# GDN mixer of a hybrid flow block on one core: k and q before v, and the gate columns as fp32 products in four column groups

## The chip, the cores and the metric

The kernel runs on one core of one Trainium2 chip. The metric is device time in microseconds (us) of one execution. Of each kernel one execution is profiled; its span runs from the first to the last instruction.

## The reference, cut to what matters

Two layers work on 512 latent and 256 context tokens of width 1024. In each layer the tokens are normalised and modulated, multiplied by one input matrix, mixed by four head groups, multiplied by an output matrix and sent through an MLP. The change lies in the first group, the bidirectional gated DeltaNet (GDN):

```
qkv = silu(dwconv_centred(concat([q, k, v]), conv_w))      # 5 taps, per channel
q, k, v = split(qkv, 3)
g = -exp(a_log) * softplus(a + dt_bias);  beta = sigmoid(b)
q, k = l2norm(q), l2norm(k)                                 # per head
# per chunk of 64 tokens: a = strict(kbeta @ k.T * decay), solve (a + I) sol = rhs, then a scan over chunks
```

So q, k and v are 256 columns each of the input product, and the gates are 16 columns (a, b) here and 16 more (input and forget gates) of the mLSTM group, which the same 32-column product makes.

## The kernel before, in words

Activations lie transposed: 128 channels on the partitions, 768 tokens along them (256 context, 512 latent). Every large product is written as three fp32r products of split operands: the weights as `whi` and `wlo`, the activations as `hhi` and `hlo` (`gemm`, `gemm_pair`; all matmuls go through the helper `mm`, L181). A block of 128 output columns takes, for 8 slices of the 1024 inputs and 2 segments of tokens (256 and 512), 3 products each. `wload` brings a weight block into one of two `wst` buffers by a DMA of the SP queue, and `wsplit` splits it, in two halves, on ACT (`whi`, L184) and DVE (`wlo`, L187).

A layer's front runs in this order of the program. `modulated` makes the eight `hhi`, `hlo` pairs from X on DVE and ACT. `gemm_pair` multiplies the gates (32 columns, out 32 partitions) and the first k block (128 columns) side by side, slice by slice, as the pairs come. The gates are copied out of PSUM, transposed by six matmuls (L639), biased, multiplied by a table of signs (L187, the constant `sgn`) and sent through a softplus in some twenty short DVE instructions on tiles of 128x192 (L649 to L664). Then a loop handles the blocks in the order k0, v0, k1, v1, q0, q1: product into two PSUM banks, copy into a padded temporary `ta` (two buffers, its borders cleared by POOL, L694 to L696), five taps (one ACT, four DVE, L190), sigmoid (one DVE, three ACT), a multiplication, and for k and q a norm over each head (`unit_rows`: square, product with `blk64`, logarithm, exponential, multiplication). At each block the next block's weights are loaded and split.

Then, for each of six chunk pairs s, `gdn_pre` builds the decays and the k by k and k by q products (`gq`), `gdn_inv` inverts a triangular matrix by five doubling steps, each a chain of small matmuls (`t`, `yt`) and DVE instructions (`T`, `Y`, `Z`), `gdn_kt` prepares keys and brings v in (`vkT`, from `vf`), and `gdn_scan` runs two steps of the scan (`rps`, `yps`, `sps`, `ops`). Behind that in program order stand the other groups' products: sk, sq, sv, the gMLP's v, lk, lq, later lv (`gemm`, `gemm_tok`), and the preparation of the mLSTM (`mb`, `aRp`, `Mt`).

What sets the order: outside one marked block late in the layer, a planner puts the instructions on each engine's queue when the program is built. It takes what is ready by its own estimate, oldest in program order first. On the chip each queue is then worked through in that fixed order, and a waiting instruction holds back those behind it. The PSUM has four general banks (`ps`) and some named ones (`gi`, `go`, `gs`). The weight splits take turns among buffers named in `wset`: two halves in `wsp`, two in `gd` (tags Y1 and Nh, later used by the inverse), and from L760 on `wsp` alone.

Of the kernel before, what the change touches and what calls it, by code (L numbers as in the profile page):

```python
# [24 lines left out]
EPS = 1e-6  # L25
NEG = -1e30
GAP = NT + 2
P1 = [1, 0, 5, 4, 3, 2]
MIXK = (4, 5, 0, 1, 6, 7, 2, 3)
ALL = ((0, 256), (256, 512))  # L30
# [13 lines left out]
def go(t):  # L44
# [2 lines left out]

_LAYOUT = (
    ("ident", 128), ("blk64", 128), ("triA", 128), ("triB", 128), ("fwd", 128), ("rev", 128), ("rot", 128),
    ("d4", 4), ("d4q", 8), ("nlo", 2), ("csel", 8), ("sgn", 32), ("eps", 1), ("odg", 64), ("half", 2),  # L50
    ("gmask", 128), ("up", 128), ("lw", 128), ("sel2", 256), ("lvl", 384),
    ("cos", 512), ("sin", 512), ("selP", 128), ("ind", 512),
)
_OFF = {}
# [9 lines left out]
def constants():  # L64

    c = np.zeros((128, NCONST), np.float32)

    def put(name, a):
        o, w = _OFF[name]
        c[:a.shape[0], o:o + w] = a  # L70

    p = np.arange(128)
    same = (p[:, None] // 64) == (p[None] // 64)
    le = p[:, None] <= p[None]
    ge = p[:, None] >= p[None]
    lo_half = p < 64
    put("ident", np.eye(128))
    put("blk64", same)
    put("triA", same & np.where(lo_half[None], le, ge))
    put("triB", same & np.where(lo_half[None], ge, le))  # L80
    put("fwd", le)
    put("rev", ge)
    rot = np.zeros((128, 128))
    for h in range(2):
        for i in range(32):
            rot[64 * h + 32 + i, 64 * h + i] = -1.0
            rot[64 * h + i, 64 * h + 32 + i] = 1.0
    put("rot", rot)
    t = np.arange(SEQ)
    inv = np.power(np.float32(10000.0), -np.arange(16, dtype=np.float32) / np.float32(16)).astype(np.float32)  # L90
    ang = np.concatenate([(t // 64).astype(np.float32)[:, None] * inv, (t % 64).astype(np.float32)[:, None] * inv], 1)
    ang = np.tile(ang.astype(np.float64).T, (4, 1))
    put("cos", np.cos(ang))
    put("sin", np.sin(ang))
    g = np.zeros((128, 2, 64))
    j, i = p[:, None] % 64, np.arange(64)[None]
    for s in range(2):
        d = (p[:, None] >= 64) ^ bool(s)
        ok = np.where(d, i <= j, i >= j)
        g[:, s] = np.where(ok, 0.0, NEG)  # L100
    put("gmask", g.reshape(128, 128))
    put("up", np.where(p[None] >= p[:, None], 0.0, NEG))
    put("lw", np.where(p[None] <= p[:, None], 0.0, NEG))
    r = np.arange(64)
    half, k8 = r // 32, r % 32
    live = k8 < 8
    put("selP", live[:, None] & ((p[None] >= 64) == half[:, None]))
    sel2 = np.zeros((64, 2, 128))
    for q in range(2):
        sel2[:, q] = live[:, None] & ((r[:, None] % 4) == 2 * q + (p[None] >= 64))  # L110
    put("sel2", np.tile(sel2.reshape(64, 256), (2, 1)))
    put("d4", live[:, None] & ((r[:, None] % 4) == np.arange(4)[None]))
    put("d4q", (k8 < 16)[:, None] & (half[:, None] == np.arange(8)[None] // 4)
        & ((r[:, None] % 4) == np.array([0, 2, 1, 3] * 2)[None]))
    put("nlo", np.where(np.stack([k8 // 4 == 1, k8 // 4 == 3], 1), -1.0, 0.0))
    c[64:128, _OFF["nlo"][0]] = np.where(k8 // 8 == 1, -1.0, 0.0)
    c[64:128, _OFF["ind"][0]:_OFF["ind"][0] + 512] = (k8[:, None] < 16) & (k8[:, None] % 8 == np.arange(512)[None] // 64)
    lv = [np.where((j // 2 == i // 2) & (j != i), -1.0 / 1024.0, 0.0)]
    for n in range(1, 6):
        b = 1 << n  # L120
        lv.append(((j // (2 * b) == i // (2 * b)) & (j // b != i // b)) / 1024.0)
    put("lvl", np.concatenate(lv, 1))
    cs = np.zeros((128, 8))
    for k in range(4):
        cs[32 * k, 2 * k] = cs[32 * k + 1, 2 * k + 1] = 1.0
    put("csel", cs)
    sg = np.ones((128, 32))
    sg[:, 8:16] = sg[:, 24:32] = -1.0
    put("sgn", sg)
    put("eps", np.full((128, 1), EPS))  # L130
    put("half", np.stack([lo_half, ~lo_half], 1))
    put("odg", np.where(j == i, 0.0, 1024.0))
    return c
# [9 lines left out]
def flow_kernel(ctx, tc, t, out, dbg=None, stop=None):  # L143
    nc = tc.nc
# [41 lines left out]
    def tt(o, a, b, op, eng=None):  # L186
        (eng or V).tensor_tensor(out=o, in0=a, in1=b, op=op)  # L187
# [39 lines left out]
    def bank(c0):  # L227
        return 0 if c0 == 0 else 1
# [53 lines left out]
    def evac(dst, o, segs, rows=128):  # L282
        for c0, cn in segs:
            act_(dst[:, c0:c0 + cn], o[bank(c0)][0:rows, 0:cn], AF.Copy)
# [224 lines left out]
    def gemm_pair(w2, acts, segs, n):  # L509
# [9 lines left out]
                           start=(k == 0 and pi == 0), stop=(k == 7 and pi == 2))  # L519
        return outs  # L520

    def gemm_tok(l, c0, pairs, hk, evac):

        outs = {}
        for j, p in enumerate(pairs):
            if j % 2 == 0:
                o = ps("mmt")
            outs[p] = (o, j)
        for kc in range(2):
            st = wst.tile([128, 8, 128], F32, tag="wst", name="wst")  # L530
            sv = st.rearrange("p k n -> p (k n)").rearrange("p (k n) -> p k n", k=4)
            nc.sync.dma_start(out=sv, in_=t["w_in"][l, 512 * kc:512 * kc + 512, c0:c0 + 256]
                              .rearrange("(k p) n -> p k n", p=128))
            hv = [[x.rearrange("p k n -> p (k n)").rearrange("p (k n) -> p k n", k=2) for x in q] for q in wsplit(st, 128)]
            for hf in range(2):
                hi, lo = hv[hf]
                for p in pairs:
                    o, j = outs[p]
                    for k in range(2):
                        kk = 4 * kc + 2 * hf + k  # L540
                        ahi, alo = hk[kk]
                        for pi, (w, a) in enumerate(((hi, ahi), (hi, alo), (lo, ahi))):
                            mm(o[:, 256 * (j % 2):256 * (j % 2) + 256], a[:, 128 * p:128 * p + 128], w[:, k, :],
                               start=(kk == 0 and pi == 0 and j % 2 == 0),
                               stop=(kk == 7 and pi == 2 and (j % 2 == 1 or p == pairs[-1])))
        for p in pairs:
            o, j = outs[p]
            evac(p, o[:, 256 * (j % 2):256 * (j % 2) + 256])
# [51 lines left out]
    for l in range(DEPTH):  # L600
# [19 lines left out]
        def z3(name, dt=F32):  # L620
            return zp.tile([128, NT], dt, tag="z3", name=name, bufs=6)

        ahead = [wload([win[:, C_AB:C_AB + 16], win[:, C_IF:C_IF + 16]]), wload([win[:, C_GK:C_GK + 128]])]
        h = modulated(l, 0, ALL, nrm, tp)
        del nrm
        xd = dp.tile([8, 128, NT], F32, tag="xd", name="xd")
# [2 lines left out]

        def temp(tag, w=GAP + 4):  # L630
            return tp.tile([128, GAP + 4], F32, tag=tag, name=tag, bufs=1 if tag == "tc" else 2)


        zg = temp("ta")
        o, o_k0 = gemm_pair(ahead, h, ALL, (32, 128))
        evac(zg[0:32], o, ALL, 32)
        o = ps("gatesT")
        for p in range(NP):
            T.transpose(o[:, 32 * p:32 * p + 32], zg[0:32, 128 * p:128 * p + 128], ident[0:32, 0:32])  # L639
        wb = z3("wb")  # L640
        ysp = z3("ysp")[:, 0:384].rearrange("p (x s g) -> p x s g", x=2, s=6)
        y, sp = ysp[:, 0], ysp[:, 1]
        u = temp("tb")[:, 0:192].rearrange("p (s g) -> p s g", g=32)
        w = temp("tc")[:, 0:192].rearrange("p (s g) -> p s g", g=32)
        tt(y, o[:, 0:192].rearrange("p (s g) -> p s g", g=32), bc(tokp[l][:, 0:32], 1, 6), ADD)
        tt(y, y, bc(cc("sgn"), 1, 6), MUL)
        nega = tokp[l][:, 32:40]
        act_(nega, nega, AF.Exp)
        V.tensor_scalar(out=nega, in0=nega, scalar1=-1.0, scalar2=None, op0=MUL)  # L649
# [32 lines left out]
            else:  # L682
                stt(x[:, a0:], x[:, a0:], f, e[:, a0:], MUL, MUL)

        cols = [(C_GK, C_GQ, C_GV)[which] + 128 * j for which, j in ((0, 0), (2, 0), (0, 1), (2, 1), (1, 0), (1, 1))]
        ready = {}
        for i, (which, j) in enumerate(((0, 0), (2, 0), (0, 1), (2, 1), (1, 0), (1, 1))):
            qlat = which == 1 and last
            segs = LAT if qlat else ALL
            o = gemm(None, h, segs, w2=ready.pop(i)) if i else o_k0  # L690
            if i < 5:
                ready[i + 1] = wload([win[:, cols[i + 1]:cols[i + 1] + 128]])
            raw = temp("ta")
            G.memset(raw[:, 0:2], 0.0)  # L694
# [8 lines left out]
            act_(acc[:, a0:], raw[:, a0:GAP], AF.Copy, scale=prm[l][:, cw:cw + 1])  # L703
            for tp_ in range(1, 5):
                stt(acc[:, a0:], raw[:, a0 + tp_:GAP + tp_], prm[l][:, cw + 6 * tp_:cw + 6 * tp_ + 1], acc[:, a0:], MUL, ADD)
            e = temp("tb")[:, 0:GAP] if i % 2 else gd.tile([128, 1024], F32, tag="at", name="e", bufs=2)[:, 0:GAP]
            sigmoid_(acc[:, a0:], e[:, a0:])
            tt(acc[:, a0:], acc[:, a0:], e[:, a0:], MUL)
            if len(unit) > 2 - 1:
# [1 line left out]
            if which < 2:  # L711
                act_(e[:, a0:], acc[:, a0:], AF.Square)
                unit.append((acc, e, a0, 0.125 if which else None))
        while unit:
            unit_rows()

# [40 lines left out]
                act_(glq[hp, :, :, f, :], o[hp, q:48:2].rearrange("p (s t h) -> p s t h", s=6, t=2), AF.Exp)  # L757


        wset[:] = [(wsp, "whi", "wlo")]  # L760
        mix = [None] * 8
        O = [xm.tile([128, NT], F32, tag="xm", name="O") for _ in range(2)]
        for x in O:
# [235 lines left out]

        gdn_pre(0)  # L1000
        gdn_inv(0)
        gdn_kt(0)
        gdn_pre(1)
        gdn_inv(1)
# [632 lines left out]
```

## Time and profile before

| what | value |
|---|---|
| median of 3 runs | 1955.21 us (1955.19 to 1955.52) |
| profiled execution | 1955.14 us, span 1953.4 us, mean granted TensorE clock 0.977 |
| TensorE matmul (PE) | 1874.8 us busy, 96% of the span |
| VectorE (DVE) | 1201.8 us, 62% |
| ScalarE (ACT) | 757.4 us, 39% |
| GpSimd (POOL) | 104.6 us, 5% |
| front of layer 0, first products to the mLSTM's preparation | about 45 to 325 us |
| front of layer 1 | about 1155 to 1400 us |

PE is the matrix engine's matmuls, PEld its weight loads, which run beside them. A busy PE isn't PE at its peak, since matmuls are pipelined and a recorded duration overlaps the next one; the distance from one start to the next tells what a matmul really costs. Idle time of an engine is given with what ended it.

### The profile page before, as it was taken

What the parts mean: (1) busy time and instruction counts of PE and PEld (TensorE: products, weight loads), DVE (VectorE), ACT (ScalarE), POOL (GpSimd) and SP (SyncE); (2) the same over time, 40 slices, a digit from 0 to 9 for tenths busy, and PEclk for the clock granted to TensorE, in tenths of its full rate; (3) what the DMA queues carried; (4) which work ended last, traced back from release to release, by engine and by line L of the source; (5) the groups of instructions that cost most, each with busy time, mean ns of one, the idle gap of its engine ahead of it and who ended that gap; (6) DMA issues with size and microseconds to landing.
All of it is one profiled execution on the core that took longest, in us unless ns stands there. A gap on an engine that the chain in (4) does not pass through costs nothing.

```text
span 1953.4 us, 34015 instructions
## 1 busy us (share of the span) xinstructions
PE 1874.8 (96%) x14131; PEld 1536.4 (79%) x14131; DVE 1201.8 (62%) x2221; ACT 757.4 (39%) x1530; POOL 104.6 (5%) x169
## 2 busy tenths in 40 slices
PE   5999999999899999999999999999999999999998
PEld 3877778778777888888888878677777778888887
DVE  3978885666769557435535349798676754444443
ACT  4652343555524312313213236434255543333242
POOL 0021110000000000000000000211100000000001
PEclk8999999999799999999999999999999999999999
DMA  8321001121464345335433222210011323333332
GB/s 310 97 52 34 13 24 34 57 65 34 147 199 129 107 131 148 116 93 151 140 87 108 78 58 55 63 35 24 23 44 33 102 81 98 97 97 97 97 97 76
DMA packets 225955, 172.56 MB, mean 88 GB/s; under 512 B 19106, under 2 KB 208008, under 8 KB 225800
## 3 DMA queue, kind: packets, MB, share of 16 engines
q1 hardware_dynamic: 219424, 153.71, 26.6%
q10 hardware_dynamic: 4680, 10.64, 1.5%
q0 software_dynamic: 1696, 6.03, 0.9%
q8 instruction: 111, 1.82, 0.4%
q14 instruction: 44, 0.36, 0.1%
HBM read 163.02 MB, written 7.34 MB: 87 GB/s over the span
## 4 chain that ended last, share of the span: by engine, by line
PE 82%; DVE 9%; ACT 3%; DMA 3%; issue 1%; POOL 1%; DVEq 0%; ACTq 0%; SPq 0%; POOLq 0%
PE mm L181 64%; PE mmt L181 3%; PE num L181 1%; PE ops L181 1%; DMA wst<-w_in 1%; PE pv L181 1%; DVE wlo L187 1%; DVE Y L187 1%; PE adaps L181 1%; PE yt L181 1%; DVE kq L190 1%; PE t L181 1%; PE pT L1353 1%; DMA adw<-ada_w 1%; PE yps L181 1%
## 5 line engine op out<-in xcount | busy, mean ns | idle before, releaser
L184 ACT ACTIVATE whi<-wst 128x512 fp32r<-128x512 f32 (+1 forms) x388 | 241.9, 627 | 683.8 <-PE mm L181 628.8
L181 PE MATMUL mm<-hhi,whi 128*128 128x512 f32 (+3 forms) x1344 | 479.5, 362 | 11.7 <-ACT hhi L184 11.0
L181 PE MATMUL mm<-hlo,whi 128*128 128x512 f32 (+3 forms) x1344 | 479.3, 357 | 1.2 <-DVE hlo L190 1.1
L181 PE MATMUL mm<-hhi,wlo 128*128 128x512 f32 (+3 forms) x1344 | 476.3, 356 | 0.0
L187 DVE TENSOR_TENSOR wlo<-wst,whi 128x512 fp32r<-128x512 f32 (+1 forms) x388 | 265.7, 689 | 312.9 <-ACT whi L184 308.5
L181 PEld LDWEIGHTS mm<-hhi,whi 128*128 128x128 f32 (+1 forms) x1344 | 252.7, 189 | 55.2 <-ACT hhi L184 14.4
L181 PEld LDWEIGHTS mm<-hlo,whi 128*128 128x128 f32 (+1 forms) x1344 | 253.9, 189 | 38.0 <-DVE hlo L190 2.3
L181 PEld LDWEIGHTS mm<-hhi,wlo 128*128 128x128 f32 (+1 forms) x1344 | 253.2, 189 | 38.6 <-issue 1.5
L181 PE MATMUL mm<-fhi,whi 128*128 128x512 f32 (+1 forms) x784 | 275.9, 352 | 0.0
L181 PE MATMUL mm<-flo,whi 128*128 128x512 f32 (+1 forms) x784 | 275.8, 352 | 0.0
L181 PE MATMUL mm<-fhi,wlo 128*128 128x512 f32 (+1 forms) x784 | 274.5, 350 | 0.0
L190 DVE SCALAR_TENSOR_TENSOR x<-mm,mod,x 128x256 f32<-128x256 f32 (+1 forms) x122 | 79.6, 653 | 139.8 <-PE mm L181 139.7
L181 PEld LDWEIGHTS mm<-fhi,whi 128*128 128x128 f32 x784 | 148.3, 189 | 21.9 <-ACT r L184 0.8
L181 PEld LDWEIGHTS mm<-fhi,wlo 128*128 128x128 f32 x784 | 148.1, 189 | 19.7
L181 PEld LDWEIGHTS mm<-flo,whi 128*128 128x128 f32 x784 | 148.4, 189 | 19.1
L190 DVE SCALAR_TENSOR_TENSOR adacc<-adw,scT,adacc 128x1024 f32<-128x1024 f32 x84 | 105.9, 1282 | 28.0 <-DMA adw<-ada_w 27.9
L187 DVE TENSOR_TENSOR flo<-r,fhi 128x768 fp32r<-128x768 f32 (+1 forms) x64 | 52.6, 825 | 39.2 <-ACT fhi L184 39.1
L184 ACT ACTIVATE fhi<-r 128x768 fp32r<-128x768 f32 (+1 forms) x64 | 47.2, 740 | 65.9 <-DVE r L187 65.9
L181 PE MATMUL mm<-mlo,whi 128*128 128x512 f32 (+1 forms) x192 | 69.7, 363 | 1.3 <-DVE mlo L187 1.3
L181 PE MATMUL mm<-mhi,whi 128*128 128x512 f32 (+1 forms) x192 | 69.5, 362 | 0.4 <-ACT mhi L184 0.4
L181 PE MATMUL mm<-mhi,wlo 128*128 128x512 f32 (+1 forms) x192 | 68.8, 359 | 0.0
L184 ACT ACTIVATE r<-mm 128x256 f32<-128x256 f32 (+1 forms) x96 | 49.1, 515 | 32.2 <-PE mm L181 32.2
(406 smaller groups left out, 2712.1 us busy)
## 6 DMA issues: line engine op xcount, KB each, us to landing
wst<-mlp_w SPq DMA_DIRECT2D x128, 512.0 KB, 3.8
adw<-ada_w SPq DMA_DIRECT2D x96, 512.0 KB, 4.1
wst<-w_in SPq DMA_DIRECT2D x44, 512.0 KB, 3.7
wst<-w_out SPq DMA_DIRECT2D x64, 128.0 KB, 3.2
xd<-x ACTq DMA_DIRECT2D x8, 384.0 KB, 3.4
x<-xd POOLq DMA_DIRECT2D x8, 384.0 KB, 5.5
xs<-x ACTq DMA_DIRECT2D x4, 512.0 KB, 7.2
wst<-w_in SPq DMA_DIRECT2D x8, 256.0 KB, 3.2
```

Source lines behind the costliest of these rows:

```text
L181: T.matmul(o, lhsT=l, rhs=r, start=start, stop=stop)
L184: S.activation(out=o, in_=i, func=f, **kw)
L187: (eng or V).tensor_tensor(out=o, in0=a, in1=b, op=op)
L190: V.scalar_tensor_tensor(out=o, in0=a, scalar=s, in1=b, op0=op0, op1=op1)
L1353: T.transpose(o[:, 256 * i + 128 * g:256 * i + 128 * g + 128], Ps[g][:, 128 * (i0 + i):128 * (i0 + i) + 128], ident)
```

## The change

The order of the blocks becomes k0, k1, q0, q1 and then v0, v1. `gemm_pair` now multiplies k0 and k1 side by side while the activations are made, and the gates follow in `gemm_groups`: plain fp32 weights, not split, against `hhi` and `hlo` read as fp32, 16 products of 32 columns for each segment, dealt out to four groups of 32 output partitions. The transposition becomes six matmuls with a table `sid`, which adds the four groups and carries the signs. The sign multiplication goes, and one small DVE instruction turns the sign of eight bias columns. The loop body becomes `project(i, o)`; blocks 0 to 3 are called before the norms end, blocks 4 and 5 (v) after `gdn_inv(0)` and before `gdn_kt(0)`.

As written, q0's weights are loaded and split twice: once ahead of the gates (`ready = {2: ...}`), and once more in `project(1)`, since `0 < i < 5` holds for i = 1; the second copy is the one used.

```diff
+PROJ = ((0, 0), (0, 1), (1, 0), (1, 1), (2, 0), (2, 1))
 P1 = [1, 0, 5, 4, 3, 2]
...
+    put("sid", np.where(p[:, None] % 32 == np.arange(32)[None], np.where(np.arange(32)[None] // 8 % 2, -1.0, 1.0), 0.0))
...
+    def gemm_groups(w, acts, segs, n):
+        outs = {0: gi("mmg"), 1: go1("mmg")}
+        for c0, cn in segs:
+            for i in range(16):
+                k, a = i // 2, acts[i // 2][i % 2]
+                g = slice(32 * (i % 4), 32 * (i % 4) + n)
+                mm(outs[bank(c0)][g, 0:cn], w[:, k], a[:, c0:c0 + cn].bitcast(F32), start=i < 4, stop=i >= 12)
+        return outs
...
-        ahead = [wload([win[:, C_AB:C_AB + 16], win[:, C_IF:C_IF + 16]]), wload([win[:, C_GK:C_GK + 128]])]
+        ahead = [wload([win[:, c:c + 128]]) for c in (C_GK, C_GK + 128)]
+        w_g = gd.tile([128, 8, 64], F32, tag="E", name="w_g")[:, :, 0:32]
+        for i, c in enumerate((C_AB, C_IF)):
+            nc.sync.dma_start(out=w_g[:, :, 16 * i:16 * i + 16], in_=win[:, c:c + 16].rearrange("(k p) n -> p k n", p=128))
...
+        first = gemm_pair(ahead, h, ALL, (128, 128))
+        ready = {2: wload([win[:, C_GQ:C_GQ + 128]])}
         zg = temp("ta")
-        o, o_k0 = gemm_pair(ahead, h, ALL, (32, 128))
-        evac(zg[0:32], o, ALL, 32)
+        evac(zg, gemm_groups(w_g, h, ALL, 32), ALL)
         o = ps("gatesT")
         for p in range(NP):
-            T.transpose(o[:, 32 * p:32 * p + 32], zg[0:32, 128 * p:128 * p + 128], ident[0:32, 0:32])
+            mm(o[:, 32 * p:32 * p + 32], zg[:, 128 * p:128 * p + 128], cc("sid"))
...
+        V.tensor_scalar(out=tokp[l][:, 24:32], in0=tokp[l][:, 24:32], scalar1=-1.0, scalar2=None, op0=MUL)
         tt(y, o[:, 0:192].rearrange("p (s g) -> p s g", g=32), bc(tokp[l][:, 0:32], 1, 6), ADD)
-        tt(y, y, bc(cc("sgn"), 1, 6), MUL)
...
-        for i, (which, j) in enumerate(((0, 0), (2, 0), (0, 1), (2, 1), (1, 0), (1, 1))):
+        def project(i, o):
+            which, j = PROJ[i]
...
-            o = gemm(None, h, segs, w2=ready.pop(i)) if i else o_k0
-            if i < 5:
+            o = o or gemm(None, h, segs, w2=ready.pop(i))
+            if 0 < i < 5:
                 ready[i + 1] = wload([win[:, cols[i + 1]:cols[i + 1] + 128]])
...
-            e = temp("tb")[:, 0:GAP] if i % 2 else gd.tile([128, 1024], F32, tag="at", name="e", bufs=2)[:, 0:GAP]
+            e = temp("tb")[:, 0:GAP] if i % 2 or i > 3 else gd.tile([128, 1024], F32, tag="at", name="e", bufs=2)[:, 0:GAP]
...
+        for i in range(4):
+            if i == 3:
+                wset[:] = [(wsp, "whi", "wlo")]
+            project(i, first[i] if i < 2 else None)
         while unit:
             unit_rows()
...
-        wset[:] = [(wsp, "whi", "wlo")]
...
         gdn_pre(0)
         gdn_inv(0)
+        for i in (4, 5):
+            project(i, None)
         gdn_kt(0)
```

## Rows read from the trace of the kernel before

**Rows 1.** The page: busy time by engine, and the chain that ended last by engine.

```profile
PE 1874.8 (96%) x14131; PEld 1536.4 (79%) x14131; DVE 1201.8 (62%) x2221; ACT 757.4 (39%) x1530; POOL 104.6 (5%) x169
...
PE 82%; DVE 9%; ACT 3%; DMA 3%; issue 1%; POOL 1%; DVEq 0%; ACTq 0%; SPq 0%; POOLq 0%
```

**Rows 2.** Busy time by stretch, both fronts (length; busy us; clock; DMA share; GB/s).

```profile
65.70:138.00 72.30, 70.71 (x433) 57.72 (x433) 57.70 (x106) 48.10 (x84) 9.86 (x25) 1.00 0.25 65
138.00:309.00 171.00, 162.72 (x2581) 126.00 (x2580) 136.72 (x262) 57.76 (x142) 27.42 (x29) 0.98 0.09 24
...
1179.00:1238.00 59.00, 57.30 (x350) 46.11 (x353) 50.97 (x99) 42.23 (x75) 8.20 (x25) 1.00 0.30 78
1238.00:1405.00 167.00, 160.85 (x2542) 122.82 (x2534) 136.25 (x266) 56.56 (x131) 27.54 (x30) 0.98 0.11 31
```

**Rows 3.** PE in order of time (start, duration): the scan's end in either layer.

```profile
308.52 0.66 PE L181 MATMUL ops<-ATb,yy 128*64 128x128 f32 x8
...
321.52 0.39 PE L181 MATMUL mm<-hhi,wlo 128*128 128x512 f32 x1
...
1404.39 0.66 PE L181 MATMUL ops<-ATb,yy 128*64 128x128 f32 x8
```

**Rows 4.** PE in order of time: products of the gates, beside the first k block.

```profile
53.22 0.28 PE L181 MATMUL mm<-hlo,whi 128*32 128x256 f32 x1
53.34 0.28 PE L181 MATMUL mm<-hhi,wlo 128*32 128x256 f32 x1
53.45 0.39 PE L181 MATMUL mm<-hhi,whi 128*32 128x512 f32 x1
53.68 0.39 PE L181 MATMUL mm<-hlo,whi 128*32 128x512 f32 x1
53.91 0.39 PE L181 MATMUL mm<-hhi,wlo 128*32 128x512 f32 x1
54.14 0.28 PE L181 MATMUL mm<-hlo,whi 128*128 128x256 f32 x1
```

**Rows 5.** PE in order of time: fp32 in four groups, the transposition, small fp32 products.

```profile
14.64 1.07 PE L181 MATMUL adaps<-adw,scT 128*32 128x256 f32 x16
...
65.63 0.65 PE L639 MATMUL gatesT<-cst,ta 32*128 32x32 f32 x6
...
324.61 0.62 PE L181 MATMUL mb<-ysp,cst 128*128 128x24 f32 x4
```

**Rows 6.** Groups of instructions by shape, 42 to 127 us (count, busy us, mean ns, idle).

```profile
L187 DVE TENSOR_TENSOR wlo<-wst,whi 128x512 fp32r<-128x512 f32 x15 | 10.3, 697 | 1.1 <-ACT whi L184 1.1
L184 ACT ACTIVATE whi<-wst 128x512 fp32r<-128x512 f32 x15 | 9.2, 625 | 7.7 <-PE mm L181 6.7 <-DVE sc L254 0.9
L190 DVE SCALAR_TENSOR_TENSOR vf<-ta,prm,vf 128x770 f32<-128x770 f32 x8 | 8.1, 1014 | 2.4 <-ACT vf L184 2.4
...
L187 DVE TENSOR_TENSOR vf<-vf,tb 128x770 f32<-128x770 f32 x2 | 1.9, 954 | 0.0
...
L288 DVE TENSOR_SCALAR vf<-vf 128x770 f32<-128x770 f32 x2 | 1.1, 555 | 0.0
```

**Rows 7.** Busy time by stretch: the beginning of the execution (columns as in rows 2).

```profile
0.00:25.00 25.00, 13.71 (x98) 8.06 (x99) 5.94 (x31) 10.24 (x29) 0.35 (x6) 0.91 0.92 335
```

**Rows 8.** PE in order of time, idle time before it in brackets: GDN and mLSTM waits.

```profile
133.52 0.89 PE L181 MATMUL gq<-kq 64*64 64x128 f32 x24
...
141.02 0.59 PE L181 MATMUL t<-Z,Nh 128*128 128x64 f16 x8 [2.21 <-DVE Z L860]
...
1240.34 0.39 PE L181 MATMUL t<-Z,Nh 128*128 128x64 f16 x8 [1.94 <-DVE Z L860]
...
1414.40 0.63 PE L181 MATMUL Mt<-cst,tc 64*128 64x64 f32 x4 [1.85 <-DVE tc L1177]
```

**Rows 9.** Busy time by stretch, around two falls of the clock (columns as in rows 2).

```profile
140.00:147.00 7.00, 5.98 (x62) 4.58 (x62) 5.03 (x10) 0.72 (x2) 1.35 (x3) 0.51 0.00 0
...
1416.80:1423.60 6.80, 6.80 (x32) 6.68 (x32) 6.64 (x13) 0.49 (x2) 0.00 (x0) 0.50 0.11 24
```

More of the change, by code (lines that the diff above doesn't have):

```diff
@@ L49 @@
     ("ident", 128), ("blk64", 128), ("triA", 128), ("triB", 128), ("fwd", 128), ("rev", 128), ("rot", 128),
-    ("d4", 4), ("d4q", 8), ("nlo", 2), ("csel", 8), ("sgn", 32), ("eps", 1), ("odg", 64), ("half", 2),
-    ("gmask", 128), ("up", 128), ("lw", 128), ("sel2", 256), ("lvl", 384),
+    ("d4", 4), ("d4q", 8), ("nlo", 2), ("csel", 8), ("eps", 1), ("odg", 64), ("half", 2),
+    ("sid", 32), ("gmask", 128), ("up", 128), ("lw", 128), ("sel2", 256), ("lvl", 384),
     ("cos", 512), ("sin", 512), ("selP", 128), ("ind", 512),
@@ L126, in constants @@
     put("csel", cs)
-    sg = np.ones((128, 32))
-    sg[:, 8:16] = sg[:, 24:32] = -1.0
-    put("sgn", sg)
     put("eps", np.full((128, 1), EPS))
@@ L683, in unit_rows @@
                 stt(x[:, a0:], x[:, a0:], f, e[:, a0:], MUL, MUL)
-        cols = [(C_GK, C_GQ, C_GV)[which] + 128 * j for which, j in ((0, 0), (2, 0), (0, 1), (2, 1), (1, 0), (1, 1))]
-        ready = {}
-        for i, (which, j) in enumerate(((0, 0), (2, 0), (0, 1), (2, 1), (1, 0), (1, 1))):
+        cols = [(C_GK, C_GQ, C_GV)[which] + 128 * j for which, j in PROJ]
+        def project(i, o):
+            which, j = PROJ[i]
             qlat = which == 1 and last
             segs = LAT if qlat else ALL
-            o = gemm(None, h, segs, w2=ready.pop(i)) if i else o_k0
-            if i < 5:
+            o = o or gemm(None, h, segs, w2=ready.pop(i))
+            if 0 < i < 5:
                 ready[i + 1] = wload([win[:, cols[i + 1]:cols[i + 1] + 128]])
```

## The prediction

> **What bounds the kernel now.** I read the page first: PE is busy for 96% of the span, and the chain that ended last is 82% PE [rows 1]. Busy time alone proves little, so I then cut the two fronts that the change touches into stretches [rows 2]. In all four PE is busy 95 to 98% and DVE 80 to 86%: PE leads, and DVE is near enough behind it to matter. Last I looked for what still stands on PE's queue when the GDN chain is done, since only that tells which of the two sets the end. In layer 0 the last products of the scan start at 308.52, and block products run on without a gap to 321.52 [rows 3]: the chain ends some 13 us before its cover does. In layer 1 the scan ends at 1404.39 [rows 3], and products for lv follow it as well. So a front ends when PE has worked off its list. PE time saved counts; a GDN chain that starts sooner counts only through fewer waits of PE.
>
> **The gates' product, PE.** Before, it's 48 products a layer (8 slices, 2 segments, 3 each). From start to start one of 256 columns takes 0.12 us and one of 512 takes 0.23 [rows 4]: 24 x 0.12 + 24 x 0.23 = 8.4 us; the mean of the true distances (53.22 to 53.91 holds two of one and two of the other) makes it 8.3. This costs PE as much as a block of 128 columns would, so putting k1 in its place beside k0 costs nothing, and k1's own 8.3 us later vanish. What comes in is the group form. The trace has it already: the 16 matmuls at 14.64 are two slices of the modulation product, four groups each, and every fp32 product is recorded as two matmuls. They take 1.07 us, of which the last four outlive their start by 0.4: (1.07 - 0.4) / 3 = 0.22 us for four at once, 256 columns wide [rows 5]. The gates need 16 products a segment, so 4 rounds of two passes: 8 x 0.22 = 1.8 for 256 columns, and 8 x 0.44 = 3.5 for 512, where I double the row. Together 5.3 us. Saved: 3.0 a layer.
>
> Weighing a rule: four groups start together in that row and the next four follow 0.22 us later, which is what one pass of 256 columns costs alone (mb's four short passes start 0.12 apart, for a tenth of the columns) [rows 5], so I take full overlap. The Trainium skill, "TensorE: Matmul & The Clock Gate", Part 3 (Packing small matmuls), measured less: three column groups gave 2.38 times and four row groups 3.07 times. By 3.07 the gates would take 32 x 0.66 / 3.07 = 6.9 us and the end would come 3.2 us later than my sum, an estimate; row and rule differ, and I go by the row.
>
> **The transposition.** Six matmuls in 0.65 us become six fp32 products, twelve passes. The nearest row is mb, four passes in 0.62 with the last one's 0.27: 0.12 each [rows 5], so 12 x 0.12 = 1.4: 0.75 more. Net on PE: -2.25 a layer, **-4.5** for both. Bounds: nothing saved if the new pieces hit a wait, and -6.0 if the transposition hides.
>
> **The doubled q0 load.** 512 KB, two ACT splits of 0.63 and two DVE splits of 0.70 more a layer; the gates' two narrow splits and the sign multiplication leave DVE. DVE gains about 0.7 us of work, on an engine with 14.6 idle in 65.7 to 138 [rows 2, 6]: 0 on the path. The used copy needs k1's buffers, free only when the pair ends, and the gates' 5.3 us are its cover; without that cover it costs PE one half's split, 0.63 + 0.70 = 1.3 a layer.
>
> **Loads.** Before the first product k0 and k1 (1024 KB) must now have come, instead of k0 and the gates (640 KB); on SP's queue the small gate loads go behind. At the start DMA is 92% busy at 335 GB/s [rows 7], so layer 0 may begin 384 / 335 = 1.1 us later; the other end is -0.4, from two narrow splits that leave DVE's queue there (an estimate, a quarter of 0.70 each and up [rows 6]). I take +0.5. In layer 1 the MLP's tail covers it. The gate loads wait there for memory of the MLP and may hold q0's load behind them on SP, which isn't needed before the pair has ended.
>
> **v behind the inverse.** On PE v0 and v1 only change places. On DVE their 8.1 + 1.9 + 1.1 = 11.1 us [rows 6] leave the way to the first `gq`, now complete at 133.52 [rows 8], and fall into the first inverse; I put that 12 to 18 us earlier. Three queues feel it: v's `ta` temporaries, and POOL's clearing of them, now stand in front of the rope tables (ACT's queue), of the gMLP weights (POOL's) and beside POOL's multiplication in `gdn_pre`; v1's sigmoid needs the `tb` that q1's norm frees; k1's copy out of PSUM waits for the gates' `ta`. Behind a late v stands `gdn_kt(0)` and so the first scan step; the 12 to 18 us are its cover.
>
> What that's worth is the waits. PE stood 2.21 us for the first inverse in layer 0 and then ran 7 us at half clock (granted 0.51, the lower of its two levels), which costs 3.4 more; in layer 1 it stood 1.94 there, and 1.85 before `Mt`, after which 6.8 us at 0.50 cost 3.4 [rows 8, 9]. Together 12.8. Such waits are places where the planned order and the chip disagree; a new order moves them and makes others. Bounds -12.8 to +11.2 (one wait with its clock, 2.2 + 3.4, new in each layer). Near the middle, since old stalls may go as easily as new ones come, with a little for the earlier chain: **-1.5**.
>
> **Sum.** -4.5 + 0.5 - 1.5 = -5.5 us. The profiled execution took 1955.14 us (span 1953.4 and 1.7 around it), 0.07 below the median of the runs, so the forecast is **1949.6 us**, 0.28% less.
>
> **The rivals.**
> 1. Forecast: PE's saving arrives, waits about as many as before. Own range 1945 to 1953. Chance 0.48. For it: the block products that outlast the scan [rows 3].
> 2. The earlier chain also removes the first inverse's waits in both layers: 2.2 + 3.4 + 1.9 = 7.5 instead of 1.5: 1943.6, and to 1939 if the fall before `Mt` goes too. For it: the waits lie where the order changes. Against: PE was filled there with sk and sq already. Chance 0.18.
> 3. The saving turns into waits: DVE, 80% busy before the change and more crowded inside the first inverse, sets the pace there, and PE finishes early only to stand. Then the -4.5 is lost and about 0.5 of loads stays: 1955.6, range 1952 to 1958. Chance 0.15.
> 4. The four groups overlap only in part at 512 columns. If a round takes a third more than in rows 5, the gates take 7.1 and 0.45 a layer is left: -0.9 + 0.5 - 1.5, 1953.2. The skill's 3.07 of above is this case. The trace speaks against it. Chance 0.04.
> 5. Slower: v's products clog PSUM. Their banks can be freed only into a `ta`, and a `ta` only by taps on a DVE that now prefers the inverse; two of the four general banks stay held, the next block's product waits, and everything on PE's queue behind it. From a wait of about 2 us on the clock falls as at 140 us: 5.6 in each layer, 11.2 - 4.0 = +7.2, 1962.3. It decides when the wait exceeds 1 us a layer beyond today's. For it: DVE at 80%. Against: 14.6 us of idle DVE time ahead of the inverse, enough for v's 11.1 [rows 2, 6]. Chance 0.13.
> 6. It doesn't do what it says: the planner may issue v's products ahead of the inverse wherever PE has nothing older ready. I expect that, in part, and the sum doesn't hang on it; that v comes late on DVE neither, leaving the -4.5 + 0.5: 1951.1. Chance 0.02.
>
> **Numbers.** A measurement of this kernel can tell about 0.2%, 3.9 us, from no change. Faster by more (below 1951.3): most of case 1 (0.38), all of 2, a little of 5 and 6 (0.02): 0.58. Slower by more (above 1959.1): case 5 and a tail of 3: 0.15. The rest 0.27. The range 1941 to 1958 holds cases 1, 3, 4, 6 and most of 2, some 8 in 10.
>
> **What would show it.** Right: 64 matmuls of 128*32 in fp32 for the gates, some 5.3 us a layer between the pair and q0; `gq` of the first chunk pair some 15 us earlier in both layers; the scan's end earlier by as much, block products outlasting it longer; `mb` earlier by 2 to 4 us. Wrong: a wait of PE above 1 us between the pair and q0, or for a `ps` bank in the first inverse; DVE idle before the first `gq`; new stretches at clock 0.5; the groups' starts further apart than 0.44 at 512 columns.

## The result, and the profile after

The changed kernel is slower: 1976.58 us median of 4 runs (1973.51 to 1978.45), ratio to before 1.0106 (95% interval 1.0089 to 1.0123), so some 21 us where 5.5 less were forecast. The profiled execution took 1975.99 us, span 1974.2, which is 20.8 more than the span before.

First the page of the changed kernel, busy time and chain by engine; they answer to [rows 1].

```profile
PE 1881.2 (95%) x14175; PEld 1533.7 (78%) x14175; DVE 1202.2 (61%) x2221; ACT 760.1 (39%) x1530; POOL 102.4 (5%) x169
...
PE 84%; DVE 8%; ACT 3%; DMA 3%; issue 1%; POOL 1%; ACTq 0%; SPq 0%; POOLq 0%; DVEq 0%
```

PE has 6.4 us more busy time though its work was meant to shrink, and it is still the chain. To see where the 20.8 us arise, cut the span at events of PE. I call a layer's front the time from the first product of the new activations to the first `Mt`; idle is the time in it in which no matmul runs.

| stretch, us | before | after | difference |
|---|---|---|---|
| start to the first product | 45.9 | 46.8 | +0.9 |
| front of layer 0 (idle in it) | 289.2 (11.6) | 296.5 (17.5) | +7.3 (+5.9) |
| between the fronts | 823.2 | 827.2 | +3.9 |
| front of layer 1 (idle in it) | 256.1 (10.8) | 265.8 (18.6) | +9.7 (+7.8) |
| `Mt` of layer 1 to the end | 539.0 | 538.0 | -1.0 |

Between the fronts the two kernels do the same, and this stretch took 823 to 829 us over all profiles of this document, so the +3.9 is scatter; the two fronts carry the loss. Not all of it is idle time. TensorE's granted clock stood at its lower level, 0.50, for 12.3 and 10.2 us of the two fronts before and for 21.2 and 20.4 us after, with PE busy for 21.3 of them before and 35.8 after. If half of that busy time is lost (an estimate), the clock took 7 us more than before, and with the 13.7 us of idle time that makes 21. The fronts together grew by 17.0: twenty `mmt` products (4 us), which stood ahead of layer 1's `Mt` before, stand behind it now.

Next, PE in order of time in the changed kernel (start, duration, idle time before it in brackets): around the end of q1's product in both layers.

```profile
101.27 1.23 PE L180 MATMUL l<-e,cst 128*128 128x258 f32 x2 [4.35 <-ACT e L183]
103.07 2.07 PE L180 MATMUL l<-e,cst 128*128 128x512 f32 x2 [0.57 <-ACT e L183]
104.93 1.35 PE L180 MATMUL gc<-gtmp,cst 128*128 128x24 f32 x6
106.22 0.67 PE L180 MATMUL glps<-gtmp,ones 64*128 64x48 f32 x4
106.81 0.58 PE L180 MATMUL mm<-hhi,whi 128*128 128x256 f32 x1
...
119.38 0.89 PE L180 MATMUL gq<-kq 64*64 64x128 f32 x24 [0.31 <-DVE kq L189]
...
309.24 0.66 PE L180 MATMUL ops<-ATb,yy 128*64 128x128 f32 x8
...
332.83 0.62 PE L180 MATMUL mb<-ysp,cst 128*128 128x24 f32 x4
...
1217.96 1.04 PE L180 MATMUL l<-tb,cst 128*128 128x258 f32 x2 [5.07 <-ACT tb L183]
1220.17 2.08 PE L180 MATMUL l<-tb,cst 128*128 128x512 f32 x2 [1.17 <-ACT tb L183]
```

q1's product has ended at 94.3. Then PE's queue holds only the norms' products (`l`) and the gates' sums (`gc`, `glps`), each behind a chain of ACT and DVE, and v0 starts at 106.81 behind all of them. The first complete `gq` is at 119.38, 14.1 us earlier than in [rows 8], as forecast. But the scan ends at 309.24 where it ended at 308.52 [rows 3]: the lead is lost on the way. And `mb` comes 8.2 us later than in [rows 5]. In layer 1, counted from the front's first product, the first `gq` starts 9.8 us sooner than before and the scan's last product 4.1 us later.

Now busy time by stretch (columns as in [rows 2]), first the changed kernel: from the end of the gates' transposition to the first `t` (the inverse's first product), from there to the first `rps` (the first full scan step), in either layer; the last two rows are the two falls of the clock.

```profile
76.81:128.29 51.48, 43.77 (x235) 33.28 (x235) 40.88 (x82) 33.19 (x55) 7.09 (x20) 0.87 0.08 21
128.29:167.60 39.31, 36.73 (x421) 28.43 (x420) 35.17 (x55) 16.40 (x31) 6.83 (x9) 1.00 0.29 70
...
1200.96:1242.69 41.73, 32.59 (x160) 22.82 (x159) 34.10 (x77) 27.02 (x47) 6.64 (x20) 0.84 0.09 26
1242.69:1284.70 42.01, 39.52 (x424) 29.36 (x423) 32.96 (x53) 19.20 (x34) 7.02 (x9) 1.00 0.25 61
...
98.70:112.40 13.70, 10.56 (x41) 7.57 (x42) 10.84 (x32) 8.45 (x16) 1.12 (x4) 0.50 0.12 35
1218.30:1232.00 13.70, 11.75 (x34) 7.12 (x32) 9.93 (x35) 8.31 (x18) 1.96 (x5) 0.51 0.14 38
```

And the same four stretches of the kernel before:

```profile
66.28:141.02 74.74, 70.94 (x434) 57.50 (x434) 60.30 (x109) 47.52 (x82) 10.74 (x25) 0.99 0.25 62
141.02:172.10 31.08, 30.92 (x372) 23.67 (x371) 24.36 (x41) 7.36 (x16) 3.99 (x5) 0.90 0.13 36
...
1179.30:1240.34 61.04, 57.40 (x362) 46.21 (x362) 53.13 (x103) 42.23 (x75) 9.32 (x25) 1.00 0.29 76
1240.34:1271.50 31.16, 31.16 (x373) 22.42 (x372) 25.82 (x47) 9.59 (x18) 5.58 (x7) 1.00 0.12 35
```

Read the length less PE's busy time. Ahead of the first `t` PE stood 3.8 and 3.6 us before the change and 7.7 and 9.1 after it, and with each stall go 13.7 us at the lower clock (in layer 0 they begin within it). From `t` to the first scan step it took 31 us in both layers, and now 39 and 42: v's taps are on DVE there (busy 24.4 us before, 35.2 after).

Last, PE in order of time where products of the gates (`mmg`) run between those of the pair; and in a second fence the busy time by stretch of `mmg` alone (length; PE, weight loads, ACT's copy; clock; DMA).

```profile
51.53 0.40 PE L180 MATMUL mm<-hhi,wlo 128*128 128x512 f32 x1
51.86 0.40 PE L180 MATMUL mmg<-hlo,w_g 128*32 128x256 f32 x1
51.87 0.62 PE L180 MATMUL mmg<-hhi,w_g 128*32 128x512 f32 x1
52.10 0.38 PE L180 MATMUL mmg<-hlo,w_g 128*32 128x256 f32 x1
52.32 0.59 PE L180 MATMUL mmg<-hhi,w_g 128*32 128x512 f32 x1
52.85 0.51 PE L180 MATMUL mm<-hhi,whi 128*128 128x256 f32 x2
```

```profile
46.00:74.60 28.60, 8.65 (x64) 2.39 (x64) 0.39 (x1) 0.92 0.48 149
```

Two products, two passes each, hold PE from 51.86 to 52.85. From start to start the gates cost 8.3 us in layer 0 and 8.4 in layer 1, as much as the old form, where 5.3 was forecast. In layer 0, 14 of the 64 passes are strewn between the pair's products and take 3.5 us (the first two of them at the lower clock); the other 50 run in one piece from 69.71 on and take 4.9.

### The profile page after: what moved, and what is told of

Read it like the earlier page. It is cut to its first block, busy times and chain, and to the rows that moved or that the text cites. A ratio compares the mean times of both kernels' runs of the same rounds, so it can differ in the third digit from the quotient of the medians.

```text
span 1974.2 us, 34102 instructions
## 1 busy us (share of the span) xinstructions
PE 1881.2 (95%) x14175; PEld 1533.7 (78%) x14175; DVE 1202.2 (61%) x2221; ACT 760.1 (39%) x1530; POOL 102.4 (5%) x169
## 4 chain that ended last, share of the span: by engine, by line
PE 84%; DVE 8%; ACT 3%; DMA 3%; issue 1%; POOL 1%; ACTq 0%; SPq 0%; POOLq 0%; DVEq 0%
PE mm L180 64%; PE mmt L180 3%; PE num L180 1%; PE ops L180 1%; DVE Y L186 1%; PE pv L180 1%; PE adaps L180 1%; PE mmg L180 1%; PE pT L1373 1%; PE yt L180 1%; PE nw L180 1%; PE t L180 1%; PE yps L180 1%; PE rps L180 1%; POOL N L186 1%
## 5 line engine op out<-in xcount | busy, mean ns | idle before, releaser
L183 ACT ACTIVATE whi<-wst 128x512 fp32r<-128x512 f32 x388 | 243.1, 631 | 677.0 <-PE mm L180 618.8
L180 PE MATMUL mm<-hhi,whi 128*128 128x512 f32 (+1 forms) x1312 | 468.8, 362 | 11.1 <-ACT hhi L183 10.1
L180 PE MATMUL mm<-hlo,whi 128*128 128x512 f32 (+1 forms) x1312 | 471.8, 360 | 0.4 <-DVE hlo L189 0.4
L180 PE MATMUL mm<-hhi,wlo 128*128 128x512 f32 (+1 forms) x1312 | 466.6, 358 | 0.8 <-DVE wlo L186 0.8
L186 DVE TENSOR_TENSOR wlo<-wst,whi 128x512 fp32r<-128x512 f32 x388 | 266.2, 691 | 321.2 <-ACT whi L183 312.1
L180 PEld LDWEIGHTS mm<-hhi,whi 128*128 128x128 f32 x1312 | 249.6, 191 | 53.0 <-ACT hhi L183 14.3
L180 PEld LDWEIGHTS mm<-hlo,whi 128*128 128x128 f32 x1312 | 251.0, 191 | 37.8 <-issue 2.5
L180 PEld LDWEIGHTS mm<-hhi,wlo 128*128 128x128 f32 x1312 | 250.1, 191 | 37.2 <-issue 1.9
```

Of the source, the lines that this page charges most:

```text
L180: T.matmul(o, lhsT=l, rhs=r, start=start, stop=stop)
L183: S.activation(out=o, in_=i, func=f, **kw)
```

## The experiments

The times of the kernel before spread from 1954.1 to 1965.8 us over the runs of this section, so each verdict is a ratio to the runs beside it. Its median was 1955.2 us beside the changed kernel and 1959.8 to 1960.8 beside the experiments, so a difference between the changed kernel's ratio and that of an experiment is uncertain by a few us more than the intervals say. The fronts come from the one profiled execution of each kernel; in brackets stand the idle time in them and the time at the lower clock.

| kernel | ratio to before (95%) | front of layer 0 (idle; lower clock) | front of layer 1 (idle; lower clock) |
|---|---|---|---|
| the changed kernel | 1.0106 (1.0089 to 1.0123) | 296.5 (17.5; 21.2) | 265.8 (18.6; 20.4) |
| e1_banks | 1.0067 (1.0051 to 1.0082) | 294.7 (17.5; 10.4) | 265.9 (18.2; 17.0) |
| e2_one_q0 | 1.0122 (1.0095 to 1.0149) | 302.9 (18.9; 26.3) | 266.6 (19.3; 23.9) |
| e3_v_ahead | 1.0012 (0.9996 to 1.0029) | 290.5 (10.9; 14.7) | 257.7 (9.3; 17.0) |
| e4_gates | 1.0008 (0.9995 to 1.0021) | 289.0 (12.7; 12.9) | 257.3 (9.7; 13.6) |
| e5_groups_close | 0.9999 (0.9980 to 1.0018) | 285.8 (13.1; 11.7) | 251.2 (10.1; 0) |
| e6_order_alone | 1.0068 (1.0048 to 1.0088) | 290.5 (14.5; 7.3) | 267.6 (18.9; 27.2) |
| e7_two_taps_after | 1.0103 (1.0086 to 1.0119) | 297.0 (13.9; 24.8) | 264.7 (19.0; 20.4) |
| e8_two_taps_before | 0.9972 (0.9957 to 0.9988) | 286.0 (11.4; 10.2) | 250.6 (9.0; 3.4) |
| e9_v0_ahead | 1.0033 (1.0020 to 1.0047) | 295.2 (12.6; 25.1) | 258.9 (13.3; 13.6) |
| e10_close_again | 1.0011 (0.9995 to 1.0027) | 284.2 (14.2; 4.4) | 254.9 (10.1; 10.2) |
| e11_close_after | 1.0081 (1.0064 to 1.0097) | 296.8 (16.9; 23.4) | 266.8 (18.5; 27.3) |
| e12_close_v_ahead | 0.9990 (0.9976 to 1.0005) | 288.5 (10.6; 16.6) | 254.9 (9.4; 13.6) |

### Which wait holds v back: e1_banks, e2_one_q0, e3_v_ahead

The program asks for the PSUM banks of `gc` and `glps` ahead of those of v0, and they come out of the same four. That is theory A; B puts it down to the weight buffers, C to DVE.

```diff
 # e1_banks
-        o = ps("gc")
+        o = gi("gc")
-            o = ps("glps")
+            o = go1("glps")
 # e2_one_q0, and all kernels below but e6, e7, e8 and e11
-            if 0 < i < 5:
+            if 1 < i < 5:
 # e3_v_ahead: e2_one_q0, with
-        for i in range(4):
-            if i == 3:
-                wset[:] = [(wsp, "whi", "wlo")]
+        for i in range(6):
             project(i, first[i] if i < 2 else None)
...
+        wset[:] = [(wsp, "whi", "wlo")]
         mix = [None] * 8
...
         gdn_inv(0)
-        for i in (4, 5):
-            project(i, None)
         gdn_kt(0)
```

> The changed kernel, with gc and glps (the gates' cumulative sums, products of a few columns) moved from the four general PSUM banks to the named banks gi and go; nothing else. Theory A (banks given out in program order): v's product gets its banks after gc and glps, which wait for the softplus, so PE has only the norms' products on its queue behind q1. Then v0's product now runs between q1 and gc: PE's waits before the l products, 5.8 us in layer 0 and 7.0 in layer 1, fall below 2 each, the falls of the clock at 98.7 and 1218.3 go or shorten, and the time is 1952 to 1961. Theory B (weight buffers: the doubled q0 load makes v0's weights wait for q1's): no change, 1973 to 1979. Theory C (DVE sets the pace and v's product only delays the stall): 1964 to 1972, with waits before l, Eps or gq that sum up to 4 us or more a layer.

> The changed kernel without the doubled load and split of q0 (1 < i < 5). Theory A: the stall behind q1 stays, only 0.7 us a layer of DVE work and 1.25 of ACT work leave: 1971 to 1978. Theory B: v0's weights use the buffers that q0 leaves, v0's product starts at the end of q1's, and the time falls to 1952 to 1962. Theory C: 1972 to 1976.

> The changed kernel without the doubled q0 load, and with v0 and v1 in the loop behind q1, so ahead of gc, of the first gdn_pre and of the first inverse; k and q first and the new gates stay. Theory A: v's banks come before those of gc, v0 and v1 (16.6 us of products) cover the norms, no wait before l above 1 us: 1947 to 1957; the first complete gq later than in the changed kernel by 10 us or more. Theory B: the same or a little less, as the weights no longer wait. Theory C: the stall moves to Eps, gq or t with 4 us or more a layer: 1960 to 1972.

B is out as the cause of the loss: without the doubled load nothing is won. e1_banks, PE in order of time, with one row of DVE, and below it PE's five longest waits from 125 to 300 us (total us, times, longest):

```profile
101.82 0.70 PE L180 MATMUL l<-e,cst 128*128 128x258 f32 x2
...
104.45 0.40 PE L180 MATMUL gc<-gtmp,cst 128*128 128x24 f32 x2
...
1207.69 0.40 PE L180 MATMUL mm<-hlo,whi 128*128 128x512 f32 x1
1212.45 1.23 PE L180 MATMUL l<-tb,cst 128*128 128x258 f32 x2 [4.36 <-ACT tb L183]
1213.48 0.58 PE L180 MATMUL mm<-hhi,wlo 128*128 128x256 f32 x1
...
1212.74 1.28 DVE L186 TENSOR_TENSOR wlo<-wst,whi 128x512 fp32r<-128x512 f32 x2
```

```profile
PE t L180 <- DVE Z L893: 3.0, 5, 1.0
PE yt L180 <- DVE T L186: 2.3, 4, 0.8
PE t L180 <- DVE Z L878: 1.8, 1, 1.8
PE rps L180 <- DVE kt L186: 1.8, 2, 0.9
PE yps L180 <- DVE Y L189: 1.4, 1, 1.4
```

In layer 0 theory A names the place rightly: with other banks for `gc`, products of v0 stand between the `l` products, and the 5.8 us of waits before `l` shrink to 0.3. In layer 1 4.4 of 7.0 stay, and the rows show why: v0 has its banks and its first products run up to 1207.69, but the next ones need `wlo`, and DVE comes to that split at 1212.74 only, behind taps and the softplus. There DVE holds v back, much as C had it. And A's price is wrong: 7.6 us are won instead of 15 to 25 (1.0106 less 1.0067, of 1955; the medians, 1976.58 and 1973.66, differ by 2.9). By its ratio e1 takes 1968 us, which lies in C's range, and the idle time of layer 0's front is 17.5 as before the edit. It has moved into the inverse and the scan (the five waits above). e3 puts v ahead of `gc` altogether, and 18 of the 21 us are gone, with idle times of 10.9 and 9.3 us, under those of the kernel before. So v's place costs most of the time; the banks cost a few us of it, and for layer 0's idle time they decide only where it is paid.

### What the gates are worth: e4_gates, e5_groups_close, e10_close_again

```diff
 # e4_gates: e3_v_ahead, with
-PROJ = ((0, 0), (0, 1), (1, 0), (1, 1), (2, 0), (2, 1))
+PROJ = ((0, 0), (0, 1), (2, 0), (2, 1), (1, 0), (1, 1))
-        ready = {2: wload([win[:, C_GQ:C_GQ + 128]])}
+        ready = {2: wload([win[:, C_GV:C_GV + 128]])}
 # e5_groups_close, e10_close_again: e4_gates, with
-                k, a = i // 2, acts[i // 2][i % 2]
+                k, a = 7 - i // 2, acts[7 - i // 2][i % 2]
```

> The gates' new form and the pair of k blocks alone: order k0, k1, v0, v1, q0, q1, all ahead of the norms' end, no doubled load. If the gates' product and its transposition are worth what the prediction's sum says (-4.5 us of PE time) and nothing else happens: 1949 to 1953. If the gates coming behind both k blocks (some 10 us later than before) delay the decays so that PE waits for them, theory D: 1956 or more. Theories A, B and C say nothing against the first.

> The kernel of e4_gates, whose groups take the slices of the activations from the last to the first (k = 7 - i // 2), so that no product of the gates can be issued before the last slice is there, and all 32 run behind the pair. In e4_gates the products of the gates were strewn in ones and twos between those of the pair and took 8.4 us of PE a layer, where the prediction had 5.3. Theory E (products of one or two groups lose the overlap of four): 5.2 to 5.6 us a layer now, and the time 4 to 7 us below e4_gates, ratio to before 0.997 to 0.999. Rival F (the strewn products filled time in which the pair had to wait for activations): the gates take 5.3, but PE stands as much longer in the pair, and the ratio stays at 1.0008 within 0.001.

> e5_groups_close once more with more rounds, since its interval (0.998 to 1.002) can't tell it from e4_gates. By its trace the two fronts were 3.4 and 4.9 us shorter than before: 0.995 to 0.998 if that holds in every execution; 0.999 to 1.001 if other parts take it back.

e4: nothing won. The time lies in theory D's range, but D's waits aren't there: ahead of the first `t` PE stands 1.7 and 3.0 us, less than before. In e5 all 64 matmuls of layer 0's gates run in one piece; busy time of `mmg` alone:

```profile
67.65:72.95 5.30, 5.30 (x64) 1.98 (x64) 0.38 (x1) 1.00 0.70 195
```

That is the forecast's 5.3, with rounds of four 0.22 us (256 columns) and 0.43 us (512) apart; layer 1 has 5.8. So theory E holds for PE: strewn, 64 passes take 8.3 us, close, 5.3. Rival F's waits don't come: from the first product to the end of the gates' transposition layer 0 takes 27.2 us in e5 and e10 and 31.0 in e4. The fronts follow: mean of e5 and e10 285.0 and 253.1, against 289.0 and 257.3 in e4. Of these 8 us 5.6 are the gates'; the rest goes with less time at the lower clock, which differs between e5 and e10, one and the same kernel (0 and 10.2 us in layer 1). The times don't follow: 0.9999 and 1.0011 against 1.0008, so the 5.6 us come out as 0 within 4. A part of them is on record as clock: the mean granted clock over the runs is 0.975 in e4, 0.973 in e5 and 0.972 in e10, and within each of these kernels a run is 1.3 to 1.6 us longer per 0.001 less (a line through its runs), which makes 2 to 5 us (an estimate). Why the clock falls more often with close groups isn't shown. That both profiles start their first product later than e4's, by 2.8 and 3.8 us, says little: e11 and e12, with close groups too, start about as early as e4 (44.8 and 45.8 against 45.1).

### The order alone, and DVE's part: e6_order_alone, e7_two_taps_after, e8_two_taps_before

```diff
 # e6_order_alone: the kernel before, with
-        for i, (which, j) in enumerate(((0, 0), (2, 0), (0, 1), (2, 1), (1, 0), (1, 1))):
+        def project(i):
+            which, j = PROJ[i]
...
+        for i in range(4):
+            if i == 3:
+                wset[:] = [(wsp, "whi", "wlo")]
+            project(i)
         while unit:
             unit_rows()
...
         gdn_inv(0)
+        for i in (4, 5):
+            project(i)
         gdn_kt(0)
 # e7 (in the changed kernel) and e8 (in the kernel before)
-            for tp_ in range(1, 5):
+            for tp_ in range(2, 4):
```

> The kernel before with the new order alone: k0 beside the gates as before, then k1, q0, q1, and v0, v1 behind the first inverse; the gates' old form, no doubled load. Theory D (the late gates are the cause: softplus 10 us later, so gc, so the banks for v): the gates are done at 20 us after the first product again, gc is free by the end of q1's product, waits before l under 2 us a layer, ratio 0.998 to 1.003. Theory C (DVE sets the pace before the first inverse, whatever PE's order): idle time of PE from the first product to Mt 16 us or more in layer 0 (11.6 before), ratio 1.005 to 1.010.

> The changed kernel with two of the four taps on DVE left out in all six blocks (12 instructions of 1.02 us a layer, 8 of them in the k and q blocks). Left out: part of the convolution. Theory C: the waits before l fall by 4 us or more a layer and the clock's falls there shorten: 10 to 20 us less than the changed kernel, ratio 1.000 to 1.005. Theory A alone (only the queue behind gc matters): gc comes earlier too, as softplus and taps share DVE, but v's product then covers all; the same time, so this run tells C from neither A nor C, and has to be read against the next. If neither holds: less than 4 us.

> The kernel before with the same two taps left out, for comparison. If PE sets the pace in the kernel before, as the prediction has it: 0 to 4 us less, ratio 0.998 to 1.000. If DVE sets it there too: 8 us or more less, ratio below 0.996.

e6: the order alone costs 0.68%, some 13 us, over D's range. It lies in C's, but the 16 us of idle time that C wanted in layer 0 aren't reached (14.5). In layer 0 early gates help as D said (front 290.5, +1.3), in layer 1 they don't (+11.5). The longest waits of PE in layer 1 (e6_order_alone):

```profile
PE gc L182 <- DVE gtmp L188: 3.8, 1, 3.8
PE t L182 <- DVE Z L865: 3.7, 2, 2.3
```

There q0 and q1 have latent tokens only, so their products are shorter, and PE reaches `gc` before the softplus is done, early gates or not.

e7 takes C apart. Here it is, from the transposition to the first `t` and on to the first `rps`, in either layer:

```profile
76.70:119.80 43.10, 41.42 (x256) 33.10 (x256) 37.01 (x77) 34.44 (x59) 7.53 (x20) 1.00 0.17 44
119.80:153.70 33.90, 30.62 (x400) 23.53 (x399) 28.44 (x46) 13.51 (x27) 7.30 (x9) 0.94 0.20 52
...
1199.10:1238.10 39.00, 32.52 (x168) 23.75 (x168) 29.55 (x70) 27.07 (x49) 6.70 (x17) 0.87 0.10 28
1238.10:1277.10 39.00, 35.41 (x402) 26.97 (x401) 29.75 (x48) 16.51 (x29) 8.25 (x9) 0.95 0.26 65
```

DVE has 24 instructions and 12 us of busy time less in the whole kernel. The waits before `l` go as C said, to 0 and 0.7 us. In layer 0 the first `t` comes 8.4 us sooner and the scan ends at 297.67 instead of 309.24, and still the time is the same (1.0103 against 1.0106): PE now stands before `rps`, `t` and, in layer 1, `gc`, and layer 0's front spends 24.8 us at the lower clock instead of 21.2. So C is right on the waits before `l` and wrong on what they are worth: a chain that runs ahead of PE's products wins nothing. The same two taps taken from the kernel before give 5.5 us (0.9972), between the two expectations: DVE has some share there, too.

### Cover: e9_v0_ahead, e11_close_after, e12_close_v_ahead

Theory G: ahead of the first `t`, PE needs products of its own for as long as the chain of DVE and ACT runs. Before, v0, k1, v1, q0 and q1 stood there (five blocks of 8.3 us in layer 0); after the change q0 and q1 alone, and v where the banks let it.

```diff
 # e9_v0_ahead: e2_one_q0, with
+        project(4, None)
         while unit:
             unit_rows()
...
         gdn_inv(0)
-        for i in (4, 5):
-            project(i, None)
+        project(5, None)
         gdn_kt(0)
```

e11 is the changed kernel and e12 is e3, both with the edit of e5.

> Between the changed kernel and e3_v_ahead: v0 is projected ahead of gc, v1 behind the first inverse; no doubled load. Theory G (cover: what counts is how much product time stands on PE's queue between the gates and the first inverse beside the chain of DVE and ACT; every stall there also costs a fall of the clock): 8.3 us more cover than the changed kernel, so PE's idle time from the gates' transposition to the first t falls from 7.7 and 9.1 us to under 4 a layer, no half clock there, and the ratio is 1.002 to 1.006, as v1 still lies in the inverse. If the place of v1 on DVE inside the inverse costs most (theory H), the first rps comes 36 us or more after the first t (31 before) and the ratio stays at 1.006 to 1.010.

> The changed kernel with the groups' slices from the last to the first, so that the gates' products run close together. Theory E: 3 us a layer less of PE time for the gates, the gates done 3 us earlier, ratio 1.006 to 1.009 instead of 1.0106. By theory G a stall between the gates and the first t stays, 5 us or more a layer, moved at most: the cover is the same.

> e3_v_ahead (k and q first, v behind them in the loop) with the groups close. If theory E's 3 us a layer add to e3: ratio 0.996 to 0.999, like e10. The order of blocks (k, q, v against k, v, q) then makes no difference as long as v stands ahead of gc.

e9, the same four stretches:

```profile
78.40:131.40 53.00, 49.57 (x319) 39.43 (x319) 47.74 (x91) 38.88 (x64) 6.67 (x20) 1.00 0.15 35
131.40:166.40 35.00, 34.43 (x390) 26.92 (x389) 27.53 (x48) 11.88 (x25) 7.24 (x11) 0.90 0.17 51
...
1199.60:1248.40 48.80, 43.68 (x284) 34.34 (x284) 44.17 (x91) 34.43 (x61) 9.55 (x22) 1.00 0.16 38
1248.40:1278.40 30.00, 30.00 (x359) 21.23 (x358) 27.36 (x50) 11.97 (x24) 8.06 (x11) 1.00 0.26 76
```

One block of cover put back: idle ahead of the first `t` is 53.0 - 49.6 = 3.4 and 5.1 us (7.3 and 10.0 in e2_one_q0, which lacks only this), the clock stays at 1.00 there, the way to the first scan step takes 35 and 30 us, so H is out, and 1.0033 lies inside G's range; layer 1's 5.1 lies over its 4. One thing doesn't fit G: in this profile layer 0's front stays at 295.2 us, since later, shorter waits leave 25.1 us of it at the lower clock. In e11, with no more cover, PE stands 6.0 and 8.9 us ahead of the first `t`, as G had it. Its ratio, 0.25% under the changed kernel's, is within E's range, but the medians are the same (1976.95 and 1976.58), so that gain isn't shown. e12 is the best of the series but for e8, which leaves out two taps; its interval holds 1, so no version that does the whole work is shown to beat the kernel before.

## Why the prediction was wrong

**What bounds the kernel.** Right, and it decided the case: PE works off a list, and a chain that starts sooner only counts through PE's waits. The first complete `gq` came 14.1 us sooner and the scan's end not at all; in e7 even more lead bought nothing, and in e6, a slower kernel than before, layer 0's scan ended 14 us sooner, counted from the first product.

**The gates.** The overlap was right: 0.22 and 0.43 us per round of four, 0.22 and 0.44 taken. The sum's 5.3 was not, since it took the 16 products of a segment as one piece. The planner strews the early ones into the pair, where one or two products at a time leave the other groups empty: 8.3. So the -3.0 a layer was 0. The transposition cost 1.3 as against 1.4. Alone, the gates' part is +0.08% (e4), not -4.5 us. Rival 4 had the loss and the wrong cause: the groups overlap fully when four of them run. The Trainium skill's factor for four packed row groups, 3.07 ("TensorE: Matmul & The Clock Gate", Part 3, Packing small matmuls), which by the prediction's estimate makes 6.9 us, fits neither arrangement here: 5.3 close, 8.3 strewn.

**The doubled load.** Costed at nothing; e2 wins nothing without it. **Loads.** +0.5 was taken; the first product starts at 47.0 us on average in the eleven profiles with the new gates and at 45.4 in the three with the old: +1.5, over the bound of 1.1, though the single profiles scatter from 44.6 to 48.8.

**v behind the inverse: the step that failed.** "On PE v0 and v1 only change places" was the error. Their products were what PE did while DVE and ACT worked on k, q and the gates. With them moved, PE met the waits at `l` (5.8 and 7.0 us) and 13.7 us of half clock in either layer. The term for waits, -1.5 with a bound of +11.2, took one new wait of 2.2 us a layer with 3.4 for the clock; measured, idle time alone grew by 5.9 and 7.8, and the lower clock took some 7 more. The rows to see it were there: PE was busy for 70.7 of 72.3 us in that stretch [rows 2]; v0, v1 and also k1, which now runs beside k0, were to leave it, three blocks of 8.3 us, while DVE's 57.7 us there would lose only v's 11.1. That leaves 45.8 us for PE and 46.6 for DVE.

**The rivals.** Rival 5 had the sign, and PSUM as a part of the cause; but it let v clog the banks inside the inverse, where in layer 0 `gc` and `glps` kept v out of them ahead of it (e1). Its step from a wait of about 2 us to a fall of the clock doesn't hold in its own rows: behind the 1.94 us at 1240.34 the clock stays at 1.00, behind the 1.85 before `Mt` it falls. Rival 3 was near in mechanism (PE finishes early only to stand) and placed the stall inside the first inverse too. That v would fill PE ahead of the inverse (rival 6) happened only from 106.81 on.

**The parts together.** The order alone costs 13 us, the gates alone 2, both 21: the missing 6 would be in layer 0's front (+1.3 and -0.2 alone, +7.3 together), where the gates' later end delays `gc`, and `gc` delays v. e1 and e6 break this link from either side: in both the waits before `l` in layer 0 are gone, and their ratios agree (1.0067 and 1.0068). But e1's front of layer 0 stays at 294.7, in e7 the same waits go with the link untouched, and 6 us is little more than the before kernel's medians differ; so the link is argued rather than shown.

What stays open: why close groups lower the mean clock, and how much of the loss in layer 1 is DVE's (its split of v0's weights in e1) beside PE's missing cover. Other work as cover (sk's or sq's products ahead of the inverse) wasn't tried.

## What to carry to other kernels

Before a product is moved away from a stretch, add up what its engine has left to do there while the chain beside it runs, in that stretch alone and for each layer, since a block over fewer tokens covers less. In an in-order queue ask also which buffers the moved step shares with what is asked for earlier in the program: v waited for banks that two tiny products held a claim on. Products that win by running side by side must be issued side by side; an order that takes whatever is ready tears them apart.

## What the runs showed of the hardware

Two fp32 products of 32 columns, one over 256 and one over 512 tokens, took 0.99 us when issued between others (51.86 to 52.85). Where all four groups run without a break, a product's share is 2 x 0.22 / 4 = 0.11 us over 256 tokens and 2 x 0.43 / 4 = 0.22 over 512, 0.33 for the two. The two strewn products do run side by side (their first passes start at 51.86 and 51.87), but in two of the four groups, and the other two stand empty. A smaller part is the change itself: from the last product of the pair to the first of the gates it is 0.33 us (51.53 to 51.86), 0.1 more than the 0.23 of 512 columns; between the 32- and 128-column products of [rows 4], both split, no such step is seen. And a stall of 5.1 us cost about as much again in its wake: in layer 1 PE stood before `l` until 1217.96, and from 1218.30 the clock was at 0.51 for 13.7 us, in which PE was busy for 11.75, so some 5.9 us were lost (an estimate, half of it).
